# Hybrid encoder on one core: order in which product banks are returned, other banks for the output projection, prompt rows loaded ahead of the keys, keys loaded once and copied on chip

## The chip, the cores and the metric

The kernel runs on one core of a Trainium2 chip. The core has TensorE (PE: matmuls; its weight loads are listed as PEld), VectorE (DVE), ScalarE (ACT), GpSimd (POOL) and SyncE (SP, which issues DMAs). The metric is device time in microseconds (us) of one execution. Tiles are named by their slot class and number: `q`, `c`, `h`, `d`, `s` are slots in SBUF (15 of 4096 bytes a partition, 4 of 4352, 61 of 2048, 2 of 2304, 33 of 64), `a`, `u`, `b`, `c` are 8 PSUM banks of 2048 bytes (3, 2, 2, 1) in the first part of the kernel, and `w` are 4 wide banks, two PSUM banks each, in the second.

## The reference

One layer of an encoder, run for a prompt (512 rows) and a sample (1024 rows) with the same weights; the width is 1024, everything is float32:

```python
h = _rmsnorm(x, norm_attn_g)
z = h @ w_in                          # columns: q 512, k 128, v 128, ca 512, cb 512
a_out = _window_attn(q, k, v, bias, band, attn_sink)   # 8 heads of 64, 2 key/value heads, |q-k| <= 128, sink logit
c = ca * sigmoid(cb)
c = _dwconv(c, conv_dw_w, conv_dw_b)  # 31 taps along the rows, 512 channels
c = silu(_layernorm(c, conv_ln_g, conv_ln_b))
x = x + concatenate([a_out, c]) @ w_out
h = _rmsnorm(x, norm_ffn_g)
u = _dwconv(h @ w_up, ffn_dw_w, ffn_dw_b)              # 3 taps, 2 x 2816 channels
x = x + (silu(u[:, :2816]) * u[:, 2816:]) @ w_down
y = _rmsnorm(x, norm_final_g)
```

## The kernel before

Every operand of a large matmul is split into a high and a low part (type fp32r), and each product is three matmuls: high by high, high by low, low by high. The split of a tile is a cast on ACT (the high part) and a subtraction on DVE or POOL (the low part). So a tile that PE uses passes DMA, ACT and DVE or POOL first.

The stages, by the trace's time line, in us:

- 0 to 270: the combined projection of all rows. The prompt's attention runs beside it as side work. Keys, values and queries are written to DRAM (`ksd`, `vsd`, `qsd`) and read again from there.
- 270 to 340: the output projection of the prompt (`prompt_out`, L770 to L775). `out_half` makes one half (512 columns) of one block of 128 rows: 24 matmuls into a bank `u`, then L775 adds the block's rows of x, which `load_x` (L143) brings. In before, the rows are loaded when a block's first half is started in the program. Beside it, the scores of the sample's attention begin (L624: two matmuls for a bank of scores, against a key tile of 128 partitions x 1024; L628 is VectorE's step on them). `load_kv` loads the keys: each of four key tiles holds the same 64 partitions twice, and each half is a DMA of its own (L810). `h2` is then made from the sums (L823, transposes L248).
- 340 to 660: the prompt's up projection (`ffn_step`; L289 to L291 into banks `u`, the three taps L930 on ACT and L926 on DVE, gate L946 to L950). The rest of the sample's attention and its convolution are side work, advanced by costs (`pace`) between the up tiles. The convolution's taps are taken one at a time by DVE (L326), a number of them (the table `LOFF`, one entry for each of three sums) by ACT (L317) and POOL (L318).
- 660 to 760: the sample's output projection, by the same `out_half`; the table `OB` names the classes of its banks. `conv_norm` (L729, L744) makes the convolution's half of its input, `turned` (L1070) turns the sums for the next stage.
- 760 to 1190: the sample's up projection, as seven products for each 128 channels over sums of quarter matrices (L1139 to L1141, sums L1020 and L1023, gate L1255 to L1276). `split_up(j, i)` makes the split for product i of channel group j (cast L1125, subtraction on POOL).
- 1190 to the end: the down projection, again seven products, in the order 1, 2, 5, 6, 7, 4, 3 (L1468 to L1470), each of 11 steps over the 2816 channels. A product fills three wide banks, `pd[0]` and `pd[1]` from its first step, `pd[2]` from its third on. `evacuate` takes them, in that order, into sums in SBUF (L1490, L1020), and `pd.clear()` gives them back. The last product is finished row block by row block (L1534 to L1551).

What sets the order: in the first 760 us a scheduler places the instructions of the emitted program on each engine by their priority and by what is free; in the later part the order of SP and PE is the order of the code (a manual schedule), the other engines still being placed. Slots and banks are taken from a free list (`Slots.tile`): of the free ones that fit, the first of the smallest; one given back goes to the end. A slot that is handed out again makes its new writer wait for its last reader. Engines work strictly through their queues.

Of the kernel before, what the change touches and what calls it, by code (L numbers as in the profile page):

```python
# [9 lines left out]
F32 = mybir.dt.float32  # L10
# [5 lines left out]
P = 128  # L16
# [3 lines left out]
HD = 64  # L20
NH = 8
NKV = 2
# [21 lines left out]
CLO, CD = 0.6, 0.65  # L44

NOFF = 4
LOFF = (5, 5, 5)
LEADIN = 8
PH = 544

# [3 lines left out]
WOP, WOA, DW, DW2 = 1, 5, 2, 2  # L54
NE = 2
YN = 2
OB = "uc"
NW = 16
BL = 9
SA = 4  # L60
# [40 lines left out]
def tile_hybrid_encoder(ctx: ExitStack, tc: tile.TileContext, xs, rel_bias, norm_attn_g, w_in,  # L101
                        attn_sink, conv_dw_w, conv_dw_b, conv_ln_g, conv_ln_b, w_out, norm_ffn_g,
                        w_up, ffn_dw_w, ffn_dw_b, w_down, norm_final_g, onehot, laid, outs):
    nc = tc.nc
# [11 lines left out]
    use = dict(step="aub", turn="aub", conv="c", attn="au", norm="b", out="b", up="u", down="b")  # L116
# [24 lines left out]
    def load_x(G, tt):  # L141
        x = sb.tile([D])
        nc.sync.dma_start(x[:], G["x"][tt * P:(tt + 1) * P, :])  # L143
        return x
# [153 lines left out]
    ksd = dr.tile([HD, NKV, 2, 1024], F32, name="ksd")  # L298
# [68 lines left out]
    tanh_t, cpads, kt, vt = {}, {}, {}, {}  # L367
# [224 lines left out]
    blocks = [(G, b) for G in GR for b in range(G["nb"])]  # L592
# [164 lines left out]
    xr, x1, wo = {}, {}, {}  # L757
# [47 lines left out]
    def load_kv():  # L805
        for kv in range(NKV):
            kt[1, kv] = [sb.tile([1024], F32R) for _ in range(2)]
            for L in range(2):
                for half in range(2):
                    nc.sync.dma_start(kt[1, kv][L][half * HD:(half + 1) * HD, :].bitcast(F32), ksd[:, kv, L, :])  # L810
        for n in range(2):
            vt[1 + n] = [sb.tile([4, P], F32R) for _ in range(NKV)]
            for kv in range(NKV):
                nc.sync.dma_start(vt[1 + n][kv][:].bitcast(F32), vsd[:, n, kv])

    h2 = {}

# [58 lines left out]
    h1.clear()  # L876
    rbs.clear()
    use.update(attn="a", norm="b", turn="ubc")
    load_kv()
    units_of_sample = attention(8, 24)  # L880
    out = deque([prompt_out()])
    n = 0
    while out:
        if side:
            for _ in range(AP):
                if side:
                    advance(side)
            if not side:
                pace.update(late=CLO)
        advance(out)  # L890
        n += 1
        if n % SA == 0 and n > 14:
            next(units_of_sample)
    drain(convs)

# [108 lines left out]
            side.append(sample())  # L1004
        ffn_step(k)
    h2.clear()
    use.update(out=OB, turn="b")
    pace.update(rate=RE)
    drain(side)

# [6 lines left out]
    L, R = slice(0, NT), slice(NT, W2)  # L1017
# [92 lines left out]
    def split_up(j, *which, apart=False):  # L1110
        if j >= NJ:
            return
        for i in which:
            if i == 7:
                held = third_sum.pop(j)
                src = held[:]
            else:
                src = block_up(j, *{1: (0, 0), 2: (0, 1), 6: (0, 0), 4: (0, 1), 5: (1, 0), 3: (1, 1)}[i])
            if not apart and any(s[0][0] in "qc" for s in sb.free):
                t = sb.tile([2, NT], F32R)  # L1120
                hi, lo = Part(t, 0), Part(t, 1)
            else:
                hi, lo = sb.tile([NT], F32R), sb.tile([NT], F32R)
            ops[j, i] = hi, lo
            nc.scalar.copy(hi[:], src)  # L1125
            sub(lo[:], src, hi[:].bitcast(F32), nc.gpsimd)
            held = None
            done.add((j, i))
        for half, pair in ((0, (6, 4)), (1, (5, 3))):
            if (j, half) in uraw and all((j, i) in done for i in pair):  # L1130
                uraw.pop((j, half))
# [234 lines left out]
    split_up(2, 5)  # L1366
    value_part(0)
    first(2)
    split_up(2, 6)
    third(1)  # L1370
    split_up(2, 7)
    fifth(2)
# [189 lines left out]
    pd = []  # L1562

    def down_step(k):
        i, p = steps[k]
        load_next(8 if k == 0 else 3 if len(pr) < CAP else 0)
        make(k + (LEAD if k else 1))
        if p == 0:
            pd.extend(wide() for _ in range(2))
        hold = 5 if i == ORDER[0] else HOLD  # L1570
        if p == hold:
            pd.append(wide())
        for tt in range(4):
            mm_down(pd[tt // 2][:, (tt % 2) * NT:(tt % 2 + 1) * NT], i, p, tt)
        hl[i, p] = None, hl[i, p][1]
        if p >= hold:
            for q in range(p + 1) if p == hold else (p,):
                for tt in (4, 5):
                    mm_down(pd[2][:, (tt % 2) * NT:(tt % 2 + 1) * NT], i, q, tt)
                hl.pop((i, q)), hp.pop((i, q))  # L1580
        if p == NPAIR - 1:
            evacuate(i, pd)
            pd.clear()
        if i == 7 and p == 4:
            load_x1(0, 0)
        if i == 7 and p == 8:
            with_x("o11", 0, 0)
        if i == 4 and p == 2:
            load_x1(1, 1)
            fins.append(sb.tile([D]))  # L1590
            nc.sync.dma_start(fins[0][:], norm_final_g.partition_broadcast(P))
            nc.scalar.activation(fins[0][:], fins[0][:], AF.Identity, scale=D ** 0.5)
        if i == 4 and p == 4:
            with_x("e", 1, 1)
        if i == 4 and p == 6:
            load_x1(0, 1)
        if i == 4 and p == 8:
            with_x("o12", 0, 1)
            load_x1(1, 0)
# [52 lines left out]
    zs, half = [], sm(1)  # L1652
# [105 lines left out]
```

## Time and profile before

| | us |
|---|---|
| runs | 1527.93, 1533.1, 1537.3 (median 1533.1) |
| profiled execution, its own time | 1534.64 |
| its span, first to last instruction | 1532.8 |
| PE busy | 1487.8 |
| DVE busy | 1118.8 |
| ACT busy | 800.9 |
| POOL busy | 764.5 |
| mean granted clock of PE | 0.988 |

The lines in the next sections come from one profiled execution. A row of the waits is the engine and line that waited, the engine and line that released it, the us in total, how often, and the longest. A row of a time line is the start, the length, engine, line, operation, output and inputs, their shapes and how many such instructions stand together, and in brackets the idle time before it and what ended it. A row of groups is the line and its shapes with a count, then busy us and mean ns, then the idle time before. Windows are explained where they stand.

### The profile page before, as it was taken

Reading aid. Unit: us, or ns where it says so; the run is one execution under the profiler, and the core shown is the slowest. Engines: PE = TensorE matmul, PEld = TensorE weight load, DVE = VectorE, ACT = ScalarE, POOL = GpSimd, SP = SyncE. Lnnn points to the kernel's source line nnn. Section 1 sums busy time; section 2 is a strip of 40 time slices with the busy share of each in tenths; the row PEclk is TensorE's granted clock in tenths of the full one; section 3 lists DMA queues with packets and bytes.
Section 4 is the critical chain, followed back from the end, with each engine's and each line's share of the span. In section 5 each row is a group of like instructions: output and inputs, shape, how many; then the busy total and the mean of one; then the engine's idle time right before and its main releaser. Section 6 shows DMA issues by size and latency. Waiting matters only on the chain. (4 is left out here: it accounts for less than half of the span.)

```text
span 1532.8 us, 19878 instructions
## 1 busy us (share of the span) xinstructions
PE 1487.8 (97%) x6736; PEld 1222.4 (80%) x6736; DVE 1118.8 (73%) x1512; ACT 800.9 (52%) x1417; POOL 764.5 (50%) x683
## 2 busy tenths in 40 slices
PE   8999999898999999989999999999999999999998
PEld 7888778687888888868887888888888888887776
DVE  7877845549899987565867888888877855657865
ACT  6434455456767776553464444444454453443345
POOL 3454353246868876352335656555565211115556
PEclk9999999998999999999999999999999999999999
DMA  9464231833444444763223343433343473446744
GB/s 375 158 172 146 83 102 31 267 139 110 145 126 123 144 125 133 240 229 105 83 79 133 114 130 126 128 127 129 128 165 114 170 265 101 131 154 196 231 161 165
DMA packets 125521, 229.24 MB, mean 150 GB/s; under 512 B 20547, under 2 KB 45891, under 8 KB 125292
## 3 DMA queue, kind: packets, MB, share of 16 engines
q1 hardware_dynamic: 123884, 226.37, 45.5%
q10 hardware_dynamic: 1536, 1.61, 0.3%
q8 instruction: 53, 0.87, 0.2%
q14 instruction: 48, 0.39, 0.1%
HBM read 167.88 MB, written 61.10 MB: 149 GB/s over the span
## 5 line engine op out<-in xcount | busy, mean ns | idle before, releaser
L1023 DVE TENSOR_TENSOR h<-h,h 128x512 fp32r<-128x512 f32 (+1 forms) x155 | 135.3, 897 | 83.7 <-ACT h L1027 35.0
L155 POOL TENSOR_TENSOR q<-q,q 128x1024 fp32r<-128x1024 f32 x66 | 159.3, 2416 | 74.2 <-ACT q L154 46.3
L1468 PE MATMUL w<-h,h 128*128 128x512 f32 x444 | 174.3, 393 | 8.6 <-DVE q L1020 8.1
L1023 POOL TENSOR_TENSOR q<-q,q 128x512 fp32r<-128x512 f32 x82 | 116.3, 1427 | 116.5 <-ACT q L1125 116.1
L1470 PE MATMUL w<-h,h 128*128 128x512 f32 x436 | 170.3, 391 | 0.0
L1469 PE MATMUL w<-h,h 128*128 128x512 f32 x428 | 167.2, 391 | 0.0
L289 PE MATMUL u<-h,q 128*128 128x512 f32 x384 | 152.0, 397 | 0.9 <-DVE h L926 0.8
L290 PE MATMUL u<-h,q 128*128 128x512 f32 x384 | 151.6, 395 | 0.0
L291 PE MATMUL u<-h,q 128*128 128x512 f32 x384 | 151.1, 394 | 0.0
L1139 PE MATMUL w<-h,q 128*128 128x512 f32 x372 | 146.0, 392 | 2.6 <-ACT q L1125 2.2
L1141 PE MATMUL w<-h,q 128*128 128x512 f32 x372 | 146.0, 392 | 0.6 <-POOL q L1023 0.6
L1140 PE MATMUL w<-h,q 128*128 128x512 f32 x350 | 137.2, 392 | 0.0
L1027 ACT CAST h<-h 128x512 fp32r<-128x512 f32 x119 | 71.8, 620 | 123.1 <-DVE h L1023 43.7
L1023 POOL TENSOR_TENSOR h<-h,h 128x512 fp32r<-128x512 f32 (+1 forms) x36 | 48.1, 1337 | 173.6 <-ACT h L1451 119.7
L1468 PEld LDWEIGHTS w<-h,h 128*128 128x128 f32 x444 | 83.7, 189 | 28.3 <-DVE q L1020 9.8
L326 DVE SCALAR_TENSOR_TENSOR c<-d,cvw,c 128x512 f32<-128x512 f32 x128 | 96.0, 750 | 1.7
L154 ACT CAST q<-q 128x1024 fp32r<-128x1024 f32 x66 | 68.8, 1046 | 53.1 <-PE u L290 28.9
L1470 PEld LDWEIGHTS w<-h,h 128*128 128x128 f32 x436 | 82.2, 188 | 17.2
L1469 PEld LDWEIGHTS w<-h,h 128*128 128x128 f32 x428 | 80.8, 189 | 16.6
L1023 POOL TENSOR_TENSOR c<-q,c 128x512 fp32r<-128x512 f32 x46 | 73.4, 1605 | 36.4 <-ACT c L1125 36.4
L318 POOL TENSOR_TENSOR h<-h,h 128x512 f32<-128x512 f32 x58 | 75.6, 1306 | 22.6 <-ACT h L317 19.1
L289 PEld LDWEIGHTS u<-h,q 128*128 128x128 f32 x384 | 72.7, 189 | 15.9 <-issue 0.9
(445 smaller groups left out, 4006.7 us busy)
## 6 DMA issues: line engine op xcount, KB each, us to landing
q<-in_laid_w_up SPq DMA_DIRECT2D x88, 512.0 KB, 3.8
ga<-q SPq DMA_DIRECT2D x65, 256.0 KB, 2.3
h<-gap SPq DMA_DIRECT2D x57, 256.0 KB, 3.3
h<-ga SPq DMA_DIRECT2D x57, 256.0 KB, 3.3
h<-in_w_down SPq DMA_DIRECT2D x52, 256.0 KB, 3.2
q<-in_laid_w_in SPq DMA_DIRECT2D x22, 512.0 KB, 4.0
gap<-h SPq DMA_DIRECT2D x44, 256.0 KB, 3.4
q<-in_x_sample SPq DMA_DIRECT2D x15, 512.0 KB, 8.2
```

The lines of the kernel that those rows point to most:

```text
L155: (nc.vector if dve else nc.gpsimd).tensor_tensor(lo[:], raw[:], hi[:].bitcast(F32), op=ALU.subtract)
L289: nc.tensor.matmul(out, whi[:, kc, :], hi[:], start=(kc == 0), stop=False)
L290: nc.tensor.matmul(out, whi[:, kc, :], lo[:], start=False, stop=False)
L291: nc.tensor.matmul(out, wlo[:, kc, :], hi[:], start=False, stop=(kc == KC - 1))
L326: nc.vector.scalar_tensor_tensor(acc[:], src(t), w(t), acc[:], op0=ALU.mult, op1=ALU.add)
L1023: (eng or nc.vector).tensor_tensor(out, a, b, op=ALU.subtract)
L1139: nc.tensor.matmul(out, whi[:, s], hi[:], start=(start and c == 0), stop=False, **go)
L1140: nc.tensor.matmul(out, whi[:, s], lo[:], start=False, stop=False, **go)
L1141: nc.tensor.matmul(out, wlo[:, s], hi[:], start=False, stop=(stop and c == 3), **go)
L1468: nc.tensor.matmul(out, sh[:, c], th[:], start=(p == 0 and not seeded), stop=False, **go)
L1469: nc.tensor.matmul(out, sh[:, c], tl[:], start=False, stop=False, **go)
L1470: nc.tensor.matmul(out, sl[:, c], th[:], start=False, stop=(p == NPAIR - 1), **go)
```

## The change

Five edits:

1. `LOFF` (6, 5, 5): in the first of the three sums of the late convolution, for each of four channel groups, six taps go to ACT and POOL, not five.
2. `OB` "cbu" and `turn` "u": the sample's output projection takes banks of the classes c, b and u (five banks; before u and c, three), and the turns of its sums take u, no longer b.
3. The four prompt blocks are loaded before `load_kv`. A key tile is loaded once into partitions 0 to 63, and POOL copies it into 64 to 127 (`double_keys`), one tile in each pass of the loop from the eighth on. The scores of the sample are advanced from pass 20 on, before from pass 16.
4. The split for product 6 of channel group 2 takes two `h` slots, not one `q` slot with two parts.
5. The wide banks are given back in the order `pd[0]`, `pd[1]`, `pd[2]`. A list's `clear()` drops its elements from the end, so that before the order was `pd[2]`, `pd[1]`, `pd[0]`.

```diff
-LOFF = (5, 5, 5)
+LOFF = (6, 5, 5)
...
-OB = "uc"
+OB = "cbu"
...
-                for half in range(2):
-                    nc.sync.dma_start(kt[1, kv][L][half * HD:(half + 1) * HD, :].bitcast(F32), ksd[:, kv, L, :])
+                nc.sync.dma_start(kt[1, kv][L][0:HD, :].bitcast(F32), ksd[:, kv, L, :])
...
+    def double_keys():
+        for kv in range(NKV):
+            for L in range(2):
+                nc.gpsimd.tensor_copy(kt[1, kv][L][HD:P, :], kt[1, kv][L][0:HD, :].bitcast(F32))
+                yield
...
+    for i in range(4):
+        xr[i] = load_x(*blocks[i])
     load_kv()
     units_of_sample = attention(8, 24)
     out = deque([prompt_out()])
-    n = 0
+    n, doubling = 0, double_keys()
...
-        if n % SA == 0 and n > 14:
+        if n > 7:
+            next(doubling, None)
+        if n % SA == 0 and n > 18:
             next(units_of_sample)
...
-    use.update(out=OB, turn="b")
+    use.update(out=OB, turn="u")
...
-    split_up(2, 6)
+    split_up(2, 6, apart=True)
...
             evacuate(i, pd)
-            pd.clear()
+            while pd:
+                pd.pop(0)
```

Lines of the changed kernel lie nine or ten below those of the kernel before from `load_kv` on (L810 is L809, L1020 is L1029, L1125 is L1134, L1219 is L1228).

SP's queue around the loads for the prompt's output projection, before (`q_471`, `q_461`, `q_463`, `q_462` are the rows of blocks 3, 0, 2, 1; two more key DMAs, for `q_435`, stand four rows above):

```order
L601 DMA h_464_2888<-qsd_154 128x512
L601 DMA h_465_2890<-qsd_154 128x512
L791 DMA h_470_2913<-in_laid_w_out 128x512
L143 DMA q_471_2915<-in_x_prompt 128x1024
L810 DMA q_434_2752<-ksd 64x1024 x2
L810 DMA q_433_2751<-ksd 64x1024 x2
L810 DMA q_436_2758<-ksd 64x1024 x2
L143 DMA q_461_2811<-in_x_prompt 128x1024
L143 DMA q_463_2867<-in_x_prompt 128x1024
L814 DMA h_440_2768<-vsd 128x512
L791 DMA h_474_2964<-in_laid_w_out 128x512
L143 DMA q_462_2839<-in_x_prompt 128x1024
```

And in the changed kernel (`q_435`, `q_433`, `q_434` are the rows of blocks 2, 0 and 1; block 3 follows, then the other two keys, the last of them eight rows further, behind a load of the bias):

```order
L143 DMA q_435_2755<-in_x_prompt 128x1024
L791 DMA h_473_2945<-in_laid_w_out 128x512
L791 DMA h_472_2943<-in_laid_w_out 128x512
L813 DMA h_441_2767<-vsd 128x512
L813 DMA h_442_2768<-vsd 128x512
L813 DMA h_443_2771<-vsd 128x512
L791 DMA h_465_2897<-in_laid_w_out 128x512
L601 DMA h_466_2918<-qsd_154 128x512
L809 DMA q_440_2764<-ksd 64x1024
L809 DMA q_439_2763<-ksd 64x1024
L143 DMA q_433_2751<-in_x_prompt 128x1024
L143 DMA q_434_2753<-in_x_prompt 128x1024
```

The first block's rows stand behind two key DMAs in place of eight, one block's rows stay ahead of them, and two loads of w_out have moved ahead as well. On PE the third output half follows straight on the second in the changed kernel; before, six matmuls L624 stood between them.

DVE at the end of a product of the down projection, product 6, the fourth in the order, with slot and bank numbers, before:

```order
L1023 TENSOR_TENSOR h37_2024_12596<-h29_2004_12540,h5_2023_12595 128x512
L1020 TENSOR_TENSOR q4_1746_11430<-w3_54_12212,q4_1746_11430 128x1024
L1020 TENSOR_TENSOR q10_1747_11431<-w2_55_12213,q10_1747_11431 128x1024
L1023 TENSOR_TENSOR h51_2026_12600<-h43_1638_10987,h9_2025_12599 128x512
L1020 TENSOR_TENSOR q1_1748_11432<-w1_56_12272,q1_1748_11432 128x1024
```

And now:

```order
L1032 TENSOR_TENSOR h37_2029_12605<-h29_2009_12549,h7_2028_12604 128x512
L1029 TENSOR_TENSOR q4_1751_11439<-w1_54_12221,q4_1751_11439 128x1024
L1029 TENSOR_TENSOR q14_1752_11440<-w2_55_12222,q14_1752_11440 128x1024
L1032 TENSOR_TENSOR h12_2031_12609<-h4_1643_10996,h11_2030_12608 128x512
L1029 TENSOR_TENSOR q1_1753_11441<-w3_56_12281,q1_1753_11441 128x1024
```

The next product's rows on PE take the banks w0, then w1, then from the third step w2, in both. Before, w1 was the bank evacuated last; now it is the one evacuated first, and the bank evacuated last, w3, is not taken by that product.

ACT around the cast for product 6 of group 2, before (`q12_1309<-q2_5`, the last row; the slot q12 was that of `q12_1308`, a tile of the gate whose last reader is DVE's gate product):

```order
L1264 ACTIVATE c2_1304_7949<-q11_1303_7945 128x1024
L1210 COPY w1_6_7995<-w0_5_7994 128x512
L1125 CAST c3_1315_8059<-q7_7_7899 128x512
L1255 ACTIVATE q12_1308_7988<-w2_3_7816,vecs_83,fw_264 128x1024
L1125 CAST q0_1312_8042<-q2_5_7840 128x512
L1240 COPY h47_1311_8040<-w1_6_7995 128x512
L1125 CAST q5_1313_8045<-q4_6_7842 128x512
L1125 CAST q12_1309_8009<-q2_5_7840 128x512
```

And now (the cast is `h39_1313<-q8_5`, the third row; L1228 is before's L1219, which wrote h25_1292 eleven rows above the first row shown before):

```order
L1346 COPY w3_4_7825<-h50_1251_7599 128x512
L1228 COPY h56_1296_7858<-w2_3_7824 128x512
L1134 CAST h39_1313_8017<-q8_5_7848 128x512
L1228 COPY h3_1298_7875<-w3_4_7825 128x512
L1241 COPY h27_1300_7904<-w2_3_7824 128x512
L1264 ACTIVATE q7_1302_7926<-w0_1_7571,vecs_83,fw_264 128x1024
L1241 COPY h10_1301_7923<-w3_4_7825 128x512
```

The cast has moved up by seventeen instructions, from behind the gate's tiles to the first copies of the group.

## The prediction

> **What bounds the kernel now.** I read first the busy shares, then TensorE's waits over the whole run.
>
> ```profile
> PE 1487.8 (97%) x6736; PEld 1222.4 (80%) x6736; DVE 1118.8 (73%) x1512; ACT 800.9 (52%) x1417; POOL 764.5 (50%) x683
> ```
>
> TensorE (PE) is busy 97% of the span, so what a scheduling change can win is what PE loses to waits and to a low clock. The waits, longest first (us in total, how many, the longest):
>
> ```profile
> PE w L1468 <- DVE q L1020: 8.1, 4, 2.8
> PE a L624 <- DVE h L669: 3.9, 1, 3.9
> PE u L770 <- DVE q L775: 3.0, 1, 3.0
> PE u L770 <- DVE h L926: 2.9, 1, 2.9
> PE w L1139 <- ACT q L1125: 2.2, 1, 2.2
> PE a L729 <- issue: 1.6, 1, 1.6
> PE w L1468 <- ACT q L1490: 0.4, 1, 0.4
> ```
>
> Each of these has its place in the time line of PE, here with the wait in brackets:
>
> ```profile
> 301.94 0.50 PE L770 MATMUL u<-h,h 128*128 128x512 f32 x1 [3.01 <-DVE q L775]
> 369.31 0.69 PE L624 MATMUL a<-q,h 128*128 128x384 f32 x1 [3.87 <-DVE h L669]
> 657.13 0.47 PE L770 MATMUL u<-h,h 128*128 128x512 f32 x1 [2.93 <-DVE h L926]
> 1385.05 0.80 PE L1468 MATMUL w<-h,h 128*128 128x512 f32 x1 [2.82 <-DVE q L1020]
> 1433.92 0.50 PE L1468 MATMUL w<-h,h 128*128 128x512 f32 x1 [2.19 <-DVE q L1020]
> 1484.66 0.50 PE L1468 MATMUL w<-h,h 128*128 128x512 f32 x1 [2.81 <-DVE q L1020]
> ```
>
> A wait can cost more than itself. The windows right behind five of the stalls, each followed by an undisturbed one of the same work (columns: window; its length and PE's busy time, with the matmuls; PEld, DVE, ACT, POOL; granted clock; DMA share; GB/s):
>
> ```profile
> 302.00:306.00 4.00, 4.00 (x11) 3.17 (x12) 2.40 (x8) 2.65 (x8) 0.00 (x0) 0.59 0.86 328
> 310.00:314.00 4.00, 4.00 (x19) 3.28 (x19) 3.33 (x11) 3.29 (x10) 1.14 (x2) 1.00 0.80 247
> 369.00:374.00 5.00, 4.69 (x11) 3.64 (x12) 5.00 (x8) 2.03 (x5) 2.38 (x2) 0.50 0.01 3
> 380.00:385.00 5.00, 5.00 (x26) 4.23 (x25) 4.89 (x8) 1.93 (x3) 2.52 (x3) 1.00 0.30 91
> 657.00:661.00 4.00, 3.87 (x10) 3.10 (x11) 2.54 (x5) 1.26 (x3) 4.00 (x5) 0.59 1.09 380
> 672.00:676.00 4.00, 4.00 (x21) 3.32 (x20) 1.04 (x2) 2.14 (x5) 1.07 (x2) 1.00 0.03 6
> 819.00:825.00 6.00, 5.23 (x15) 3.84 (x16) 4.74 (x6) 1.88 (x4) 1.27 (x1) 0.72 0.60 217
> 826.00:832.00 6.00, 6.00 (x28) 4.92 (x27) 3.22 (x4) 2.73 (x5) 5.85 (x5) 1.00 0.56 198
> 1385.00:1388.40 3.40, 3.35 (x8) 2.67 (x9) 0.33 (x1) 1.24 (x2) 3.40 (x2) 0.54 0.13 39
> 1390.00:1393.40 3.40, 3.40 (x16) 2.82 (x15) 1.51 (x3) 0.62 (x1) 0.00 (x0) 1.00 0.63 175
> ```
>
> PE counts as busy in both windows of a pair, yet does 8 matmuls where it does 16 (0.54 against 1.00 of the clock). What is lost on top of the wait is (missing matmuls) x (window / full count): behind 302 8 x 4/19 = 1.7 us; 369 15 x 5/26 = 2.9; 657 11 x 4/21 = 2.1; 819 13 x 6/28 = 2.8; 1385 8 x 3.4/16 = 1.7. So the five places cost, waits included and what lies in both counted once: about 4.7 (302), 6.4 (369), 4.9 (657), 4.8 (819, its 2.2 us wait ending at 819.16), 4.5 (1385). The stalls at 1433.92 and 1484.66 I price at their waits. The Trainium skill, "TensorE: Matmul & The Clock Gate", Part 1, says that the clock halves after at least one idle window of about 3.4 us; by that, waits under 3.4 us would cost only themselves, and 819 and 1385 would be worth 4.5 us less. The trace disagrees: 2.82 us of waiting is followed by 0.54 of the clock, so I count the windows.
>
> **Part by part.**
>
> *Banks in the order of emptying (down projection).* Three wide banks are evacuated by L1020 in the order pd[0], pd[1], pd[2]; the next product's second bank is the last freed in before. VectorE's time line before the 1385 stall:
>
> ```profile
> 1379.65 2.34 DVE L1020 TENSOR_TENSOR q<-w,q 128x1024 f32<-128x1024 f32 x2
> 1381.92 1.95 DVE L1023 TENSOR_TENSOR h<-h,h 128x512 fp32r<-128x512 f32 x1
> 1383.79 1.21 DVE L1020 TENSOR_TENSOR q<-w,q 128x1024 f32<-128x1024 f32 x1
> ```
>
> PE wants the bank at 1385.05 - 2.82 = 1382.2; pd[0]'s evacuation is the first of the two from 1379.65 and ends near 1380.8, and pd[2]'s at 1385.0. With pd[0] as the second bank (the order rows above show it), the wait goes whole. The third bank, now pd[1], is wanted only in the product's third step, 24 matmuls after its first, and is empty when those two evacuations end, at 1382.0; the one emptied last is not wanted until a product later. The waits on L1020 and L1490 sum to 8.5; without the last, 2.8, that is 5.7, and with the 1.7 of half clock 7.4 us. The last transition I price apart, since behind it the operands are late already:
>
> ```profile
> 1506.47 0.50 PE L1469 MATMUL w<-q,h 128*128 128x512 f32 x1 [0.41 <-DVE q L1023]
> ```
>
> With 2.8 us less ahead of it PE only waits longer there; bounds 0 and 2.8, taken 0.5, near the row. Term: **-7.9**.
>
> *The prompt's rows ahead of the keys.* The first output half's sum (L775) waits for the first block's rows:
>
> ```profile
> 301.20 0.69 DVE L775 TENSOR_TENSOR q<-u,q 128x512 f32<-128x512 f32 x1 [6.99 <-DMA q<-in_x_prompt]
> 285.67 0.33 SPq L143 DMA_DIRECT2D q<-in_x_prompt  x1
> 286.67 3.65 SPq L810 DMA_DIRECT2D q<-ksd  x6
> 290.90 3.07 SPq L143 DMA_DIRECT2D q<-in_x_prompt  x2
> 283.00:289.00 6.00, 4.21 (x20) 3.05 (x19) 4.01 (x7) 3.96 (x7) 1.86 (x2) 1.00 1.05 333
> 289.00:295.00 6.00, 6.00 (x21) 4.78 (x20) 4.24 (x6) 3.27 (x7) 1.47 (x2) 0.72 1.04 246
> ```
>
> The queues are full (share above 1): 246 GB/s while the keys pass, 333 before. A key DMA of 256 KB then takes 1.07 us, a weight DMA of that size 0.79. Ahead of that block stood eight key DMAs; now two, and two more weight DMAs (512 KB of another block's rows stand ahead of it in both orders): -6 x 1.07 + 2 x 0.79 = -4.8 us. The rows land at 296.4 in place of 301.2, L775 (0.69) is done at 297.1. PE reached its wait at 301.94 - 3.01 = 298.9, behind six matmuls of L624 that now come later; without them (6 x 4/19 = 1.3 us) it wants the bank at 297.6. It is free, by half a microsecond, so 3.0 + 1.7 go; for so small a margin I take **-4.5**. Bounds: 0 (the rows as late as before) and 4.7. Late next is the second half of the first block, whose sum needs only the same rows. The Trainium skill, "SBUF — State Buffer", Door 1, says that 64 partitions reach half of the DMA's ports; by that a key load alone would go at half pace, the pair of before used both halves, two loads would take 2.1 us more, and the term would be nearer -2.4. No run here shows a lone one yet.
>
> *Keys copied on chip.* Four POOL copies of 64x1024, not in this trace. Nearest rows: half as many elements with two inputs, and 128x1024 with two:
>
> ```profile
> L692 POOL TENSOR_TENSOR q<-q,h 64x512 fp32r<-64x512 f32 x1 | 1.3, 1282 | 0.6 <-DVE q L690 0.6
> L155 POOL TENSOR_TENSOR q<-q,q 128x1024 fp32r<-128x1024 f32 x2 | 4.8, 2390 | 2.3 <-DVE h L669 1.7 <-DVE q L823 0.6
> ```
>
> So 1.3 to 2.4 us each, 2.0 taken (one input, full row), 8 us in all, in the stretch where POOL has nothing to do (0.00 busy in 302 to 306). Behind a copy that waits for its DMA stand L692 of the last prompt blocks and the small L627 copies which each sample score needs. The last key stands behind a bias load in SP's queue; PE's first use of it comes four output halves later than the scores did. Cost 0 to 3 us: 0.5.
>
> *Six offloaded taps in place of five.* Four DVE taps less, four ACT and four POOL operations more, at
>
> ```profile
> L326 DVE SCALAR_TENSOR_TENSOR c<-d,cvw,c 128x512 f32<-128x512 f32 x128 | 96.0, 750 | 1.7
> L318 POOL TENSOR_TENSOR h<-h,h 128x512 f32<-128x512 f32 x5 | 6.9, 1382 | 0.2
> 450.00:550.00 100.00, 99.25 (x471) 82.39 (x470) 93.87 (x166) 74.73 (x133) 77.48 (x65) 1.00 0.41 129
> ```
>
> 3.0 us off DVE (94% busy there), 5.5 onto POOL (77%): hidden; 5.5 us at most if POOL were late. The 369 stall stands behind a run of L326 taps ahead of L669; with the sample's scores started later and the first up group's taps interleaved, part of its 6.4 us goes: 0 to 6, taken **-3**.
>
> *Output projection on five banks, turns on u.* The 657 stall waits for a u bank held by the last up tile's taps (L926). Five banks let PE start elsewhere, and the attention parts of four halves (48 matmuls) go first. But these weights and cats come by DMA, which is full in the 657 window (1.09), so the 1.6 us of L729 may stay. Of 4.9 + 1.6: bounds 0 and 6.5, taken **-4**.
>
> *The first unpaired split.* L1125 waited for a q slot held by the gate product:
>
> ```profile
> 818.49 0.62 ACT L1125 CAST q<-q 128x512 fp32r<-128x512 f32 x1 [3.14 <-DVE q L1276]
> ```
>
> Two h slots are free far earlier; in the order rows above the cast moves from behind the gate products to right behind the first L1228 copy, seventeen ACT instructions sooner. The next candidate to be late is the cast for the seventh product, wanted later. Of 4.8: bounds 2 and 4.8, taken **-4.3**.
>
> Sum: -7.9 - 4.5 - 3 - 4 - 4.3 + 0.5 = -23.2; for new small stalls that this reshuffling makes, one such as the 2.2 us above: +2, so -21. The profiled execution took 1534.6 (span 1532.8), the median of the runs shown is 1533.1: 1534.6 - 21 = 1513.6, less those 1.5 us: **1512**.
>
> **Rivals.** About 1% is what a measurement of this kernel can tell from no change: 1517.8 and 1548.4 are its ends.
>
> 1. *Given back by VectorE.* DVE has 6 us free in 100 of the up stage. What PE wins at 302 and 369, 7.5 us, is then lost again before 650, and the drain is bound by DMA (share 1.09), so its 4 go too: 1512 + 11.5 = 1523.5. Against: by 657 DVE is at 2.54 of 4 us, so the stage ends with room on it, and side work that slips goes there. Chance 0.25, times 1518 to 1529.
> 2. *Only the banks and the split count, or not even these*: the next product's operands (L1023) are late as at 1506.47 and take the place of the bank waits. 1533.1 - 4 = 1529. Against: before 1498 no such wait stands among the longest. 0.08.
> 3. *Slower: u banks at the turns.* In the sample's output projection turns now share u with half sums that VectorE must add first. A PE stalled there for 2.9 us pays 4.9 as at 657. There are 16 halves; eight stalls are 39 us, 1512 + 39 = 1551, over the upper end; from eight on it decides. Against: DVE is busy 1.04 of 4 us at 672, so sums are added at once. 0.05.
>
> My forecast's case, 1504 to 1517, has 0.62. Faster: 0.62 and a fifth of rival 1, 0.67; same 0.28; slower 0.05. The range runs from 1504 (369 gone whole, 3.4 us more, the drain too, 2.5, and no new stalls, 2) to 1526 in rival 1.
>
> **What would show it.** L1468 <- L1020 gone from the waits but for one; the clock 1.00 behind 1385, 302 and 819; L775 no longer waiting for the prompt's rows; L1139 <- L1125 gone. A granted clock of 0.5 behind 369 or in the drain would strike those terms; a wait of L624 on a POOL copy, or L729 / L1070 on L775, would speak for what I priced near nothing.

## The result, and the profile after

| | before | changed |
|---|---|---|
| runs, us | 1527.93 to 1537.3, median 1533.1 (4 runs) | 1511.48 to 1518.03, median 1515.2 (4 runs) |
| profiled execution, us | 1534.64 | 1514.8 |
| its span, us | 1532.8 | 1513.0 |
| PE busy, us | 1487.8 | 1480.5 |
| mean granted clock | 0.988 | 0.992 |

The ratio is 0.9883, with a 95% interval from 0.9846 to 0.9921: 1.2% faster. The forecast was 1512 (1504 to 1526). In sum the two traces differ by 19.8 us, where the prediction's sum was 21. The parts are another matter.

The page of the changed kernel gives the busy times:

```profile
PE 1480.5 (98%) x6736; PEld 1216.5 (80%) x6736; DVE 1106.2 (73%) x1508; ACT 801.7 (53%) x1421; POOL 785.1 (52%) x691
```

Its waits of PE, longest first (us in total, how many, the longest; L1477 to L1479 are the matmuls L1468 to L1470 of before, L1148 is L1139, L1029 and L1032 are L1020 and L1023):

```profile
PE w L1478 <- DVE h L1032: 2.8, 1, 2.8
PE w L1148 <- ACT w L1237: 2.6, 1, 2.6
PE u L500 <- ACT h L466: 2.4, 1, 2.4
PE b L771 <- POOL h L803: 2.2, 1, 2.2
PE w L1479 <- POOL d L1032: 1.6, 1, 1.6
...
PE w L1477 <- ACT h L1460: 0.8, 1, 0.8
PE w L1477 <- DVE q L1029: 0.4, 1, 0.4
```

Of the seven waits that the prediction listed, 0.4 us is left, of the 8.1 for banks on L1020; those of L624 on L669, of L770 on L775 and on L926, of L1139 on its cast and the two smaller ones are gone. But three of the four longest are new, and each stands a little behind a place where one went:

```profile
653.75 0.80 PE L771 MATMUL b<-h,h 128*128 128x512 f32 x1 [2.25 <-POOL h L803]
835.84 0.50 PE L1148 MATMUL w<-h,q 128*128 128x512 f32 x1 [2.59 <-ACT w L1237]
1472.86 0.50 PE L1477 MATMUL w<-h,h 128*128 128x512 f32 x1 [0.82 <-ACT h L1460]
1475.15 0.50 PE L1479 MATMUL w<-h,d 128*128 128x512 f32 x1 [1.57 <-POOL d L1032]
1479.58 0.79 PE L1478 MATMUL w<-h,h 128*128 128x512 f32 x1 [2.77 <-DVE h L1032]
```

The first and the last of them halve the clock as well, here in windows behind them (columns as in the prediction's windows), beside one from the down projection without a stall:

```profile
653.70:657.10 3.40, 3.35 (x8) 2.70 (x9) 2.86 (x3) 0.05 (x1) 3.40 (x5) 0.52 0.09 34
1479.50:1482.90 3.40, 3.32 (x8) 2.65 (x9) 2.28 (x3) 1.62 (x5) 1.38 (x3) 0.50 0.20 78
1362.00:1366.00 4.00, 4.00 (x19) 3.31 (x18) 4.00 (x4) 0.40 (x1) 2.64 (x2) 1.00 0.58 196
```

Where the time went is seen best in PE's **lead**: both programs have 6736 matmuls on PE, and the lead is how much earlier the same one, counted through, starts in a trace than in the trace of before. (In the first 760 us the order of the matmuls differs, so the lead is good to about 1 us there; from 760 us on the order is the same.) For the changed kernel:

| place, in before's time | lead at its end | gained there | the prediction's term |
|---|---|---|---|
| start to 285 | 0.7 | 0.7 | 0 |
| 285 to 345, prompt's output projection | 9.1 | 8.4 | 4.5, less 0.5 for copies |
| 345 to 650, up stage with L624's stall at 369 | 13.2 | 4.1 | 3 |
| 650 to 800, drain, sample's output projection | 14.2 | 1.0 | 4 |
| 800 to 1180, sample's up projection | 16.0 | 1.8 | 4.3 |
| 1180 to 1490, down projection without its last product | 27.0 | 11.0 | 7.4 and some of 2.8 |
| last product | 19.8 | -7.2 | rest of the last transition |
| not placed | | | -2 for new stalls |

### The profile page after: what moved, and what is told of

It reads as the page before. It is cut to its first block, busy times and chain, and to the rows that moved or that the text cites. A ratio compares the mean times of both kernels' runs of the same rounds, so it can differ in the third digit from the quotient of the medians.

```text
span 1513.0 us, 19880 instructions
## 1 busy us (share of the span) xinstructions
PE 1480.5 (98%) x6736; PEld 1216.5 (80%) x6736; DVE 1106.2 (73%) x1508; ACT 801.7 (53%) x1421; POOL 785.1 (52%) x691
## 5 line engine op out<-in xcount | busy, mean ns | idle before, releaser
L1032 DVE TENSOR_TENSOR h<-h,h 128x512 fp32r<-128x512 f32 (+1 forms) x155 | 134.3, 891 | 82.9 <-ACT h L1036 36.4
L1032 POOL TENSOR_TENSOR q<-q,q 128x512 fp32r<-128x512 f32 x81 | 117.1, 1455 | 116.4 <-ACT q L1134 116.4
L1477 PE MATMUL w<-h,h 128*128 128x512 f32 x444 | 173.7, 391 | 1.3 <-ACT h L1460 0.8
L1479 PE MATMUL w<-h,h 128*128 128x512 f32 x436 | 170.1, 390 | 0.0
L1148 PE MATMUL w<-h,q 128*128 128x512 f32 x368 | 143.9, 391 | 2.9 <-ACT w L1237 2.6
L1150 PE MATMUL w<-h,q 128*128 128x512 f32 x368 | 143.7, 391 | 0.0
L1149 PE MATMUL w<-h,q 128*128 128x512 f32 x347 | 135.5, 390 | 0.0
L1032 POOL TENSOR_TENSOR h<-h,h 128x512 fp32r<-128x512 f32 (+1 forms) x36 | 48.5, 1348 | 161.9 <-ACT h L1460 109.6
L1477 PEld LDWEIGHTS w<-h,h 128*128 128x128 f32 x444 | 83.8, 189 | 19.7 <-ACT h L1460 1.2
L1479 PEld LDWEIGHTS w<-h,h 128*128 128x128 f32 x436 | 82.1, 188 | 17.1
L1032 POOL TENSOR_TENSOR c<-q,c 128x512 fp32r<-128x512 f32 x46 | 72.5, 1586 | 41.8 <-ACT c L1134 41.8
L318 POOL TENSOR_TENSOR h<-h,h 128x512 f32<-128x512 f32 x62 | 80.5, 1300 | 17.9 <-ACT h L317 15.7
L1148 PEld LDWEIGHTS w<-h,q 128*128 128x128 f32 x368 | 69.1, 188 | 18.6 <-ACT w L1237 3.0
```

The lines of the kernel that those rows point to most:

```text
L1032: (eng or nc.vector).tensor_tensor(out, a, b, op=ALU.subtract)
L1148: nc.tensor.matmul(out, whi[:, s], hi[:], start=(start and c == 0), stop=False, **go)
L1149: nc.tensor.matmul(out, whi[:, s], lo[:], start=False, stop=False, **go)
L1150: nc.tensor.matmul(out, wlo[:, s], hi[:], start=False, stop=(stop and c == 3), **go)
L1477: nc.tensor.matmul(out, sh[:, c], th[:], start=(p == 0 and not seeded), stop=False, **go)
L1479: nc.tensor.matmul(out, sl[:, c], th[:], start=False, stop=(p == NPAIR - 1), **go)
```

## The experiments

Each is one profile of one kernel, and one time (t_g has four); the kernel before, run beside them, took 1530.76 to 1535.48 us in nine runs. The lead is always against before's trace, at the same matmuls. A single profile starts with a lead of -1.2 to 1.6 at 285 from the stretch that no edit touches, and chance adds more behind it. s_banks, s_apart and s_ob run their matmuls in before's order up to 650 and differ from it only later, and yet their leads there are 1.0, 2.3 and 2.2 us, of which 1.6, 0.2 and 2.1 are gained between 285 and 345. From 1180 to the last matmul, the eight runs that keep the old order of the wide banks (s_ and a_ runs but s_banks) change by -2.6 to 1.0. So differences below about 2 us say nothing, and before's profile itself seems to be a late one by 1 to 2 us, which is then part of every lead.

### The order of the wide banks, alone and taken away

```diff
 # s_banks: the kernel before with
-            pd.clear()
+            while pd:
+                pd.pop(0)
```

> The kernel before with one edit: the three wide banks are given back in the order they are emptied. In the changed kernel PE stands 10.9 us earlier at the start of the last down product than at the end of the up stage, against before, and 7.1 us of that are lost again inside the last product. Theory A (the prediction's term): the five waits at the ends of products go for good, 7.4 us, and the last product gives back only its own 2.8; the profiled time falls by about 7.9 us. Theory B: the last product is paced by VectorE's and GpSimd's chain (sums, block finishes), which does not follow PE; the five waits go here too, PE is some 8 us earlier at the start of the last product, but the last product gives back all but about 4 us; the profiled time falls by 3 to 5 us. Rival C: the waits need the other edits to go; less than 2 us.

The lead grows by 5.3 us from 1180 to 1400, by 8.4 up to the start of the last product, and all of it is lost inside that product: the lead is 0.8 at 1180 and 0.7 at the end, and the time was 1533.88. The first half of both theories held, and of the second even B was too kind. The waits of PE in the last product of s_banks:

```profile
1491.11 0.50 PE L1468 MATMUL w<-h,h 128*128 128x512 f32 x1 [1.25 <-ACT h L1451]
1493.40 0.79 PE L1470 MATMUL w<-h,d 128*128 128x512 f32 x1 [1.56 <-POOL d L1023]
1497.83 0.79 PE L1469 MATMUL w<-h,h 128*128 128x512 f32 x1 [1.93 <-DVE h L1023]
```

These are the three instructions at which the changed kernel waits at 1472.86, 1475.15 and 1479.58. The other direction:

```diff
 # a_nobanks: the changed kernel with
-            while pd:
-                pd.pop(0)
+            pd.clear()
```

> The changed kernel with the wide banks given back in the old order. Theory A (what is won at the ends of products is given back in the last product, as in the kernel before with this edit alone, where 8.4 us came to 0): the waits of some 8 us at the product ends come back, the last product loses some 5 to 8 us less than in the changed kernel, and the end is within 2 us of the changed kernel's 1514.8. Theory B (the edit is worth 3.8 us, the difference of the two traces): the end is 3 to 5 us later.

The bank waits are back, 8.0 us in four places, and the lead inside the last product grows by 0.7 us, where it falls by 7.2 in the changed kernel. From 1180 to the end the lead changes by -0.4, against +3.8 in the changed kernel, and the time was 1520.06. So theory B here: in the company of the other edits the order of the banks is worth about 4 us of the 11 that it frees; by itself it showed none. The 3.8 lies outside the -2.6 to 1.0 of the runs with the old order, and t_x, below, has 4.1 with the new one. Why the same edit gives nothing alone is not shown.

### What paces the last product

In the last product VectorE has two kinds of work in one queue: the splits (L1032) that PE waits for, and the finishes of blocks already done (L1559, which waits for row statistics that GpSimd makes in L1548 and L1549). VectorE in the changed kernel, ahead of the last of the three stalls:

```profile
1469.55 0.75 DVE L1559 SCALAR_TENSOR_TENSOR q<-q,s,c 128x512 f32<-128x512 f32 x1 [0.99 <-POOL s L1549]
1472.07 1.76 DVE L1559 SCALAR_TENSOR_TENSOR q<-q,s,c 128x512 f32<-128x512 f32 x1 [1.77 <-POOL s L1549]
1474.49 1.16 DVE L1032 TENSOR_TENSOR h<-h,h 128x512 fp32r<-128x512 f32 x1 [0.65 <-ACT h L1036]
1476.09 1.76 DVE L1559 SCALAR_TENSOR_TENSOR q<-q,s,c 128x512 f32<-128x512 f32 x1 [0.44 <-POOL s L1549]
1477.78 1.75 DVE L1032 TENSOR_TENSOR h<-h,h 128x512 fp32r<-128x512 f32 x1
```

VectorE is idle for 3.2 us in the first, second and fourth of these rows, waiting for statistics, while the split that PE wants at 1476.8 stands behind them. Two experiments, one on this and one on another suspect, the rows of x that are added to the sums just before:

```diff
 # t_f: the changed kernel with
-    OTHER = {1: 2, 3: 3, 4: 8, 6: 9, 8: 10, 9: 11}
+    OTHER = {3: 2, 5: 3, 6: 8, 7: 9, 9: 10, 10: 11}
 # t_x: the changed kernel with
+        if i == 4 and p == 1:
+            load_x1(1, 1)
         if i == 4 and p == 2:
-            load_x1(1, 1)
...
-        if i == 4 and p == 6:
+        if i == 4 and p == 5:
             load_x1(0, 1)
```

> The changed kernel, with the six block finishes that lie inside the last product begun one or two steps later (steps 3, 5, 6, 7, 9, 10 in place of 1, 3, 4, 6, 8, 9). In the changed kernel VectorE waits 9.3 us in 8 places for GpSimd's row statistics (L1559 <- L1549), some of them ahead of operand splits that PE then waits for. Theory A (the finishes stand in the way of the splits): PE's loss in the last product falls from 7.8 to below 5 us, and the profiled time by 2 us or more unless the end after the last matmul grows. Theory B (the splits are late by their own data and the evacuations): PE's loss stays within 1 us.

> The changed kernel, with the rows of x for two of the final sums loaded one down step (about 4 us) earlier (from step 1, not 2, and from step 5, not 6, of product 4). In the changed kernel VectorE waits 3.3 us and GpSimd 4.1 us for such rows near 1438, ahead of operand splits, and PE loses 7.8 us in the last product. Theory A (rows of x late): these waits shrink by about 3 us, VectorE's chain comes earlier by about as much, and PE loses 3 to 5 us less in the last product. Theory B (the chain of block finishes on VectorE, ScalarE and GpSimd paces the last product from the evacuation on): the waits shrink but PE's loss stays within 1 us of 7.8.

t_f: the last product loses 3.9 us (lead 26.2 to 22.3), not 7.2. Of the three stalls one is left:

```profile
1479.87 0.50 PE L1478 MATMUL w<-h,h 128*128 128x512 f32 x1 [2.53 <-DVE h L1032]
```

That is theory A. The time, 1515.32, did not follow: the last matmul starts 2.4 us earlier (1504.3 for 1506.7) and the span ends 0.5 later (1513.5), because GpSimd is now full in the last stretch. The same window in t_f, and in the changed kernel:

```profile
1495.00:1505.00 10.00, 9.68 (x43) 7.70 (x41) 6.42 (x7) 5.49 (x14) 9.67 (x14) 1.00 0.39 150
```

```profile
1495.00:1505.00 10.00, 10.00 (x46) 8.29 (x45) 5.36 (x5) 4.42 (x9) 8.91 (x10) 1.00 0.55 212
```

t_x: the last product loses 6.0 us, hardly less than 7.2; the time was 1517.17. It doesn't settle its question in full, though: VectorE's waits for rows of x fell only from 5.2 to 4.2, GpSimd's from 9.7 to 5.8, while VectorE's waits for weights grew from 3.3 to 5.5 and GpSimd's waits for VectorE from 10.5 to 25.2. (A wait of GpSimd for an operand's load, 8.8 us in the changed kernel, went.) So waits mostly changed places.

Since GpSimd bounded the end of t_f, the next kernel takes work from it there:

```diff
 # t_g: t_f with
-    def finish(blk, parts, tail):
+    def finish(blk, parts, tail, dve=False):
...
-                    nc.gpsimd.tensor_tensor(out, out, fins[0][:, s], op=ALU.mult)
+                    (nc.vector if dve else nc.gpsimd).tensor_tensor(out, out, fins[0][:, s], op=ALU.mult)
...
-        finish(tt - 4 if tt > 3 else 4 + tt, (cut(o11, tt), cut(o12, tt)), False)
+        finish(tt - 4 if tt > 3 else 4 + tt, (cut(o11, tt), cut(o12, tt)), False, True)
```

> The changed kernel with the six block finishes of the last product begun later (as before: PE lost 3.2 us less, but the end after the last matmul grew by 2.9), and with the multiplication by the norm's gain in the four finishes after the product on VectorE in place of GpSimd, which was 97% busy there. If the finishes on GpSimd are the bound of the end, the growth of 2.9 us goes and the kernel is 2 to 3 us faster than the changed one, at about 1512; if the end is bound by the last matmul's own chain (square, power, scale, store), it is the same within 1 us.

GpSimd falls to 5.36 of 10 us in that window:

```profile
1495.00:1505.00 10.00, 8.78 (x39) 6.95 (x37) 6.46 (x10) 6.00 (x15) 5.36 (x9) 1.00 0.61 237
```

From the last matmul to the span's end it is 6.8 us (1503.4 to 1510.2), after 9.2 in t_f and 6.3 in the changed kernel. Of the 2.9 us by which the end had grown, 2.4 are gone, so GpSimd's finishes were the bound there. The median is 1511.96 us (1508.88 to 1512.23, 4 runs); its ratio to before is 0.9859, 0.9839 to 0.9879. Against the changed kernel's 0.9883 (0.9846 to 0.9921) that is 3 us better by the medians, but the intervals overlap. In the traces the down projection alone, from 1180 to the last matmul, gains 6.7 us on before here and 3.8 in the changed kernel (6.1 and 3.8 to the span's end).

### The split in two h slots

```diff
 # s_apart: the kernel before with
-    split_up(2, 6)
+    split_up(2, 6, apart=True)
```

> The kernel before with one edit: the split for product 6 of channel group 2 takes two h slots. Theory A (the prediction's term): the stall of 5.0 us at 819 goes and nothing comes for it; PE stands 4.3 to 5 us earlier from there to the end of the up stage. Theory B (read from the changed kernel): a second stall of about 2.9 us follows some 21 us later, where ScalarE's copy for PE stands behind another cast that waits for a slot; PE is about 2 us earlier. In both the down stage hands on what it gets, up to the last product.

Theory B; the time was 1529.48. The lead goes from 1.8 at 800 to 6.8 at 830, the whole stall of 819, and then back to 4.1 at 860, by a stall of 2.3 us at 847.73. PE's row, and ScalarE's two ahead of it, show the reason:

```profile
847.73 0.50 PE L1139 MATMUL w<-h,q 128*128 128x512 f32 x1 [2.27 <-ACT w L1228]
846.57 0.62 ACT L1125 CAST c<-q 128x512 fp32r<-128x512 f32 x1 [5.44 <-DVE q L1276]
847.10 0.58 ACT L1228 COPY w<-w 128x512 f32<-128x512 f32 x1
```

In the changed kernel the lead is 14.2, 19.1 and 16.0, and ScalarE shows the same (L1237 is before's L1228, L1285 its L1276):

```profile
834.68 0.62 ACT L1134 CAST c<-q 128x512 fp32r<-128x512 f32 x1 [5.49 <-DVE q L1285]
835.21 0.58 ACT L1237 COPY w<-w 128x512 f32<-128x512 f32 x1
```

PE waits until 835.8 for L1237, the copy out of a bank. ScalarE does nothing for 5.5 us before it, but the next instruction in its queue is a cast for a later product, into a `c` slot that VectorE's gate product (L1285) frees at 834.65. It is the same mechanism as at 819: a cast for later, ahead of work for now, waiting for a slot of the gate. The edit took away the first such cast only.

### The first 650 us: rows first, keys once, later scores, the sixth tap

```diff
 # s_x: the kernel before with
+    for i in range(4):
+        xr[i] = load_x(*blocks[i])
     load_kv()
 # s_late: the kernel before with
-        if n % SA == 0 and n > 14:
+        if n % SA == 0 and n > 18:
 # s_keys: s_late with the keys loaded once and double_keys, as in the change
 # s_xk: s_x and s_keys together
 # s_loff: the kernel before with
-LOFF = (5, 5, 5)
+LOFF = (6, 5, 5)
```

> The kernel before with one edit: the four prompt blocks are loaded ahead of the keys; the keys are still loaded twice, the scores start as before. Theory A (the order of the loads makes the stall): the rows of the first block stand behind two key DMAs, not eight, PE's wait for L775 at 302 goes, and PE is 3 to 5 us earlier by 345; the stall at 369 stays. Theory B (the keys only take the place of the rows): six key DMAs behind 2 MB of rows land some 4 us later, the scores L624 that still stand between the output halves wait for them, and PE is less than 1.5 us earlier by 345.

> The kernel before with one edit: the scores of the sample are advanced from pass 20 of the loop on, not 16. Theory A (the start of the scores makes the later stall): the wait of L624 at 369 for VectorE goes or shrinks, PE gains 4 us or more between 345 and 380, and the wait for the prompt's rows at 302 stays. Theory B (the stall at 369 goes in the changed kernel by the sixth offloaded tap or by another edit): 369 keeps its 6.3 us within 1.5.

> The kernel before with the keys loaded once and copied by GpSimd, and with the scores from pass 20 on; the rows of the prompt stay behind. Theory A (bytes): 1 MB less in the queue ahead of the first block's rows, 4.3 us at 246 GB/s; the wait at 302 falls from 3.0 us to below 1 and its half clock goes. Theory B (64 partitions take half of the ports, so that four loads into one half take as long as eight into both): the rows come no earlier and the wait at 302 stays within 1 us. On the copies: 1.3 to 2.4 us each by the prediction; 1.04 in the changed kernel.

> The kernel before with the prompt's rows first, the keys once and copied, and the scores from pass 20 on; the taps, the banks of the output projection, the split and the order of the wide banks as before. Alone, rows first gave 8.9 us by 345 and nothing at 369; keys once with the later scores gave 4.8 us by 345 and left a 2.7 us wait at 364. Theory A (the two together make the whole gain of the first 400 us): PE is 11 to 13 us earlier at 380 and nothing is left of the long wait at 369. Theory B (the sixth offloaded tap is needed for 369): a wait of 2.5 us or more with half clock stays between 355 and 375, and PE is 7 to 9 us earlier at 380.

> The kernel before with six offloaded taps in the first late sum. Theory A (the tap clears VectorE's run ahead of L669): the wait at 369, 3.9 us and 2.4 of half clock, falls below 2 us in all. Theory B: it stays within 1.5 us of its 6.3, and the edit moves PE by less than 1 us anywhere.

Lead of each at five places (the lead at 285 is what the run brought along):

| | 285 | 345 | 380 | 650 | end | time, us |
|---|---|---|---|---|---|---|
| s_x | -0.8 | 8.1 | 7.3 | 8.0 | 5.3 | 1529.26 |
| s_late | 1.1 | 2.0 | 2.8 | 2.4 | 1.2 | 1533.40 |
| s_keys | -0.4 | 4.4 | 4.6 | 4.2 | 0.4 | 1534.20 |
| s_xk | -0.9 | 8.0 | 7.2 | 7.4 | 8.2 | 1526.43 |
| s_loff | -0.2 | 2.5 | 2.5 | 3.8 | 6.1 | 1528.45 |
| changed kernel | 0.7 | 9.1 | 12.4 | 13.2 | 19.8 | 1514.80 |

**The rows.** Rows first makes the whole gain up to 345: 8.9 us alone, 8.9 with the keys, 8.4 in the changed kernel; some 2 us of each can be chance, by the runs with before's order. In the changed kernel the first block's rows are issued at 284.05 and land at 291.7; VectorE waits half a microsecond for them, and PE takes the bank as the sum ends:

```profile
282.79 1.15 SPq L809 DMA_DIRECT2D q<-ksd  x2
284.05 1.65 SPq L143 DMA_DIRECT2D q<-in_x_prompt  x3
291.80 0.69 DVE L775 TENSOR_TENSOR q<-u,q 128x512 f32<-128x512 f32 x1 [0.56 <-DMA q<-in_x_prompt]
292.55 0.50 PE L770 MATMUL u<-h,h 128*128 128x512 f32 x1
294.00:298.00 4.00, 4.00 (x19) 3.29 (x18) 1.23 (x3) 0.00 (x0) 1.03 (x1) 1.00 1.03 315
```

**The keys.** s_keys is theory A too: with 1 MB less ahead of them the rows land 3.9 us earlier (VectorE's L775 at 297.3 for 301.2), and PE's wait for it falls from 3.0 to 0.3 us; s_late, which differs from s_keys in the keys alone, keeps it at 3.4. With the rows first this adds nothing up to 345. The copies take 1.04 us each, with idle time of GpSimd around them, and no wait of PE names one:

```profile
289.65 1.04 POOL L818 CAST q<-q 64x1024 fp32r<-64x1024 f32 x1 [5.09 <-DMA q<-ksd]
302.55 1.03 POOL L818 CAST q<-q 64x1024 fp32r<-64x1024 f32 x1 [5.29 <-DMA q<-ksd]
```

**The stall at 369.** No single edit takes it away. Later scores alone gain 0.8 us between 345 and 380, not 4, and the wait for the prompt's rows stays at 3.4 us; its theory A falls. A wait of 2 to 2.7 us stays, only its name changes; here the rows of s_x, s_late, s_xk and s_loff, in this order:

```profile
362.94 0.77 PE L289 MATMUL u<-h,q 128*128 128x512 f32 x1 [2.01 <-DVE h L928]
```

```profile
365.98 0.77 PE L289 MATMUL u<-h,q 128*128 128x512 f32 x1 [2.73 <-DVE h L926]
```

```profile
360.19 0.77 PE L289 MATMUL u<-h,q 128*128 128x512 f32 x1 [2.73 <-DVE h L935]
```

```profile
367.33 0.50 PE L680 MATMUL a<-h,h 128*128 128x512 f32 x1 [2.27 <-ACT h L668]
```

In the first three PE waits for the first up tile's taps on VectorE, and with the sixth tap alone for a cast of the attention. In the changed kernel all edits are there and the waits in that place are 0.8 and 1.4 us. Theory B of s_xk held (the lead at 380 is 7.2, not 11 or more), and s_loff lies between its two: its wait in that place is 2.3 us for 3.9, but by the lead it gains nothing from 345 to 380. Of its 6.1 at the end, 2.7 come before 345, most of it within chance, 1.3 from 380 to 650 and 2.0 from 650 to 760, where the prediction had no term for it. That the tap is what is missing in s_xk is so far a conclusion by exclusion: s_xk and the changed kernel differ up to 380 only in it, but a scheduler places every instruction anew after such an edit.

### Other banks for the output projection

```diff
 # s_ob: the kernel before with
-OB = "uc"
+OB = "cbu"
...
-    use.update(out=OB, turn="b")
+    use.update(out=OB, turn="u")
```

> The kernel before with one edit: the sample's output projection on the banks c, b and u, its turns on u. Nothing changes before 650. Theory A (the prediction's term): the waits of 8.2 us in 650 to 668 shrink by about 4 us. Theory B (the drain is bound by the DMAs and by the last splits of w_out, as the waits of the changed kernel there for the loads of the convolved rows and for L803 on GpSimd suggest): they shrink by 2 us or less. Rival C (turns on u wait for sums): new waits of 1 us or more behind 720.

Theory B: the lead is 2.2 at 650 and 3.0 at 760, and the time was 1532.4. PE is idle for 5.4 of 18 us there (647.5 to 665.5), and for 6.3 in before (650 to 668, not the 8.2 that the expectation names). The wait for L926 went, and others came up:

```profile
653.58 0.47 PE L770 MATMUL u<-h,h 128*128 128x512 f32 x1 [1.53 <-ACT h L689]
659.84 0.50 PE L771 MATMUL u<-h,h 128*128 128x512 f32 x1 [1.00 <-POOL h L803]
662.40 1.09 PE L729 MATMUL a<-ident,h 128*128 128x128 f32 x4 [1.83 <-issue]
```

Even the 0.8 us between 650 and 760 can't be put down to the edit: without it the lead changed there by -1.6 in s_x, 0.5 in s_late, 2.0 in s_loff and 2.5 in s_xk. No turn waited for a sum of the output projection in s_ob, nor in the changed kernel: the one turn that waits there (L1079 at 755.18, 1.1 us) waits for VectorE's subtraction L1032, which reads a bank of the turns.

## Why the prediction was right, and where not

The time was right, to 3 us. It was right because errors of both signs cancelled, so that the closeness is luck; five of its steps were off.

- **The price of a stall** (wait plus missing matmuls behind it) held. The lead rose by 4.6 us where s_banks lost the stall at 1385, priced at 4.5, and by 5.0 in s_apart at 819, priced at 4.8. The waits named with these prices went.
- **Banks in the order of emptying, term 7.9, got 3.8.** The first part was right: 11.0 us by the start of the last product, more than the 7.4, since the last wait went as well. The step that failed is the bound on what is given back: "bounds 0 and 2.8, taken 0.5" spoke of the last transition alone. The last product gave back 7.2, more than that transition brought. I had read the 0.41 us wait at 1506.47 as a small leftover; it was the sign that the product's splits stand in VectorE's queue behind finishes, with no slack. A slack checked on operands before 1498 says nothing of the product behind it. That product gave back most of what PE had won inside the down projection, and with its finishes begun later, in t_f, 3.9 in place of 7.2. What was won ahead of 1180 it passed on: s_apart has a lead of 4.4 at its start and 5.1 at the end, a_nobanks 13.9 and 14.6. Rival 2's mechanism was at work there, if only there.
- **The first unpaired split, term 4.3, got 1.8.** "The next candidate to be late is the cast for the seventh product" named the wrong one. It was a copy for PE behind the next cast of the same kind.
- **Output projection on five banks, term 4, got 1.0** with the sample's part: 2.5 up to 760, and 1.5 lost again around a turn (lead 15.7 at 760, 14.2 at 800). How much of the 2.5 is the banks' is open: alone they brought 0.8, and s_xk gained 2.5 without them. Rival 1 had said that the drain would give nothing; it came out nearer to that, by the waits for L803 and for the loads of the convolved rows.
- **The prompt's rows, term 4.5, got 8.4.** The mechanism was right and the size was not. The rows landed at 291.7, not 296.4: not only the bytes ahead shrank, the load was also issued 6.9 us sooner (284.05 for 290.90). And the term priced only the stall at 302, while the two smaller ones near 288 and 298 went too. Part of that is chance: the one at 288 had halved the clock in before's profile and did not in s_banks, which is the same program up to there (below). s_banks and s_ob gain 1.6 and 2.1 from 285 to 345 with this edit absent, so the edit's own part is nearer 6.5 than 8.4. The small margin was real: PE takes the bank at 292.55, right as the sum ends, and in a_nobanks, the same program up to there, it waited 1.4 us for it.
- **The stall at 369, term 3, got 3.3** by 380 and 4.1 by 650. Rival 1, that VectorE gives back in the up stage what was won before it, did not come: the lead grew from 12.4 at 380 to 13.2 at 650.
- **Rival 3**, turns that wait for u banks, didn't come.
- **The copies** cost 1.04 us, under the lower bound of 1.3, which was that of an instruction with two inputs.

## What to carry to other kernels

A stall that goes uncovers what stands behind it in the same in-order queue: before counting it in full, follow the queue of the engine that releases it for one more stage, to the next instruction that waits. Once PE was early enough here, the finishing work bound the end of the program (t_f): there, work for now has to stand ahead of work that waits for statistics, and the engine that finishes has to have room. And count a slack where the time is to arrive, not where it is won.

## What the runs showed of the hardware

**The same wait costs differently from run to run.** The kernel before and s_banks are the same program up to the down projection. In both PE waits 1.19 us for L738, and behind it the clock was 0.61 in one profile and 1.00 in the other; first before, then s_banks:

```profile
288.35 0.33 PE L744 MATMUL a<-ident,h 128*128 128x128 f32 x1 [1.19 <-DVE h L738]
288.30:291.70 3.40, 3.35 (x12) 2.74 (x13) 3.26 (x4) 2.28 (x6) 1.91 (x3) 0.61 1.06 280
```

```profile
288.99 0.33 PE L744 MATMUL a<-ident,h 128*128 128x128 f32 x1 [1.19 <-DVE h L738]
288.90:292.30 3.40, 3.31 (x17) 2.82 (x18) 3.27 (x5) 2.33 (x6) 1.96 (x3) 1.00 1.07 297
```

In a_nobanks a wait of 2.64 us kept the full clock, and in t_g one of 1.99 us did not:

```profile
1369.86 0.50 PE L1477 MATMUL w<-h,h 128*128 128x512 f32 x1 [2.64 <-DVE q L1029]
1369.80:1373.20 3.40, 3.34 (x15) 2.77 (x16) 1.60 (x3) 1.24 (x2) 3.40 (x2) 1.00 0.13 37
```

```profile
833.69 0.50 PE L1148 MATMUL w<-h,q 128*128 128x512 f32 x1 [1.99 <-ACT w L1237]
833.60:837.00 3.40, 3.31 (x9) 2.66 (x10) 3.12 (x3) 1.06 (x3) 2.14 (x2) 0.60 0.61 201
```

So a stall of 1 to 3 us costs itself, or itself and some 1 to 3 us more (12 matmuls for 17 in 3.4 us here are 1.0; the prediction's windows gave 1.7 to 2.9), and its length doesn't tell which. The Trainium skill ("TensorE: Matmul & The Clock Gate", Part 1) says that the gate watches a window of 3.4 us that runs free of the program; that it is free running agrees with the change from run to run. That it takes an idle window of this length to halve the clock does not agree with the 1.19 us.

**Loads into 64 partitions.** By the trace's landing times, three lone key loads of 256 KB in s_keys land at 293.5, 295.1 and 296.3, so 1.2 to 1.6 us apart, and the 512 KB of a block into 128 partitions behind them after 1.0 us. Three loads of 256 KB into 128 partitions (`vsd`) land 0.6 us apart a little earlier. In before the two halves of a key came 1.0 to 1.3 us apart as well, one after the other. So here a load into half of the partitions took about the time of one of twice the bytes into all, and dropping the second half saved it. (The times are not firm: in the changed kernel the second and third of the three blocks behind the keys land 1.2 and 2.5 us after the one before.) The Trainium skill ("SBUF — State Buffer", Door 1) says that 64 partitions reach half of the ports; the half pace agrees, while the loss of 2.1 us that I had worked out from it rested on two halves overlapping, and they didn't.
